# A hybrid decoder layer: input projection from a transposed copy of the input, with the norm factor applied to the projections

## The chip, the cores and the metric

The kernel runs on one core of a Trainium2 chip. A core has five engines with their own instruction queues: TensorE (PE; its weight loads are listed as PEld), VectorE (DVE), ScalarE (ACT), GpSimd (POOL), and SyncE (SP), which here issues most of the DMAs. They wait for each other through semaphores. The metric is the device time of one execution in microseconds (us), taken as the median of several runs.

## What is computed

One decoder layer on 1040 tokens (16 meta tokens ahead of 1024 inputs) of width 1024. The part that matters here is its beginning:

```python
def rmsnorm(x, g):
    y = x * lax.rsqrt(jnp.mean(x * x, axis=-1, keepdims=True) + EPS)
    return y * g

h = concatenate([meta, x], axis=1)
a = rmsnorm(h, ln_mix_pre)
proj = a @ w_in                         # 1024 x 3584
dq, dk, dv, hq, hf, hi, hg = split(proj)
y_diff = diff_attention(dq, dk, dv, ...)   # 4 heads, 128 columns of each kind a head
y_hgrn = hgrn2(hq, hf, hi, hg, ...)        # 4 heads, 128 columns of each kind a head
mix = concatenate([y_diff, y_hgrn]) @ w_out
h = h + rmsnorm(mix, ln_mix_post)
...                                     # convolutional FFN, then the output
```

The factor `rsqrt(mean(x*x) + EPS)` is one number for each token, and `g` one number for each of the 1024 input columns. So `(x * r * g) @ w` is the same as `((x * g) @ w) * r`, with `r` a factor for each token.

## The kernel before

**Precision.** Large products are made from numbers split in two: a high part (type fp32r) and the remainder. A product of two such numbers takes three matmuls: high by high, low by high, high by low. The normed, transposed input lies in SBUF as `ahi` and `alo`, 128 input columns on the partitions, eight such slices `k`, tokens along the row. A weight tile (128 columns of `w_in`) is loaded in two halves of 128x512 and split into `wh` and `wl`.

**Tokens.** They are divided into nine blocks (16 and eight times 128), and these into three groups of 272, 384 and 384 tokens (`GROUPS`). One projection of one kind for one group is 24 matmuls: eight slices by three products.

**Order.** TensorE executes its instructions strictly in the order in which the program writes them (`manual_schedule`). The other engines' instructions are placed by a scheduler ahead of time, which moves ready work forward; within the stretch in which `state["ordered"]` is true, each instruction of DVE, ACT and POOL is pinned behind the one written before it on its engine. `interleave` mixes a dense stream of projection matmuls with a side stream by estimated costs.

**The head** (lines 792 to 971). This is what happens before the loop over the heads:

- Token blocks are loaded as they are, tokens on the partitions. `pre_stat` (ACT) squares and sums each row and makes the factor by Ln and Exp; `pre_scale` (DVE) multiplies in the factor and the gain row `gb`, which two matmuls with a row of ones spread over the partitions (line 835). Blocks 4 and 5 are scaled on ACT and POOL (`far_block`).
- `pre_turn` transposes a block on TensorE, eight 128x128 pieces into two PSUM banks; `pre_hi` (ACT) copies them out as the high part, `pre_lo` (DVE) forms the remainder.
- `Kinds` does the projections of the first group of `dq`, `dk` and `dv` and the second group of `dq` in a hand-written order, among the transposes of blocks 3 to 5. `head0(1)` and `head0(2)` do the rest, with the transposes of blocks 6 to 8 and the four matmuls of the relative-position bias tables (`bias_tables`, line 353) as side streams.
- As a projection of a group ends, its `ev_...` function evacuates the PSUM bank. `ev_q` and `ev_k` split `q` and `k`: two ACT copies into the high parts of the halves, then two DVE remainders. `ev_v` (ACT) copies to `vt`, and `to_nat` later transposes `vt` back to tokens on the partitions.

**After the head** (lines 983 to 988) the loop over four head pairs mixes the projections of an HGRN head (`hf`, `hq`, `hi`, `hg`) with the attention of one head, then the projections of the next attention head with the work of the HGRN head. There `ev_f`, `ev_q`, `ev_i` and `ev_g` of `hgrn_in` evacuate; the transposes of `hi` and `dv` (`flush`) come 8 or 14 matmul steps after the group's end. In this loop two PSUM banks take the projections in turn. Output projection and FFN follow.

## Time and profile before

| | |
|---|---|
| median of 3 runs | 1275.59 us (1275.04 to 1276.89) |
| span of the profiled execution, first to last instruction | 1275.4 us |
| mean granted TensorE clock | 0.999 |
| weight load of the first `hf` matmul (the head is over) | 57.58 us |
| input and weights in flight by DMA | about 2 to 19.5 us |

The profiled execution's own time is known as its span; the median of the runs lies 0.2 us above it. In the profile a row in order of time gives start and duration in us, then engine, line, operation, written tile, read tiles, shapes and a count of merged instructions; in brackets stands the idle time of that engine before the row and what ended it. Most DVE, ACT and POOL instructions go through a helper at line 58 and are told apart by their tiles. Matmul durations include a pipeline tail that overlaps the next matmul, so their cost is read from start to start.

### The profile page before, as it was taken

To read this page: it belongs to the slowest core of one execution; us is meant where nothing else is said; L and a number is where in the kernel's file an instruction comes from. 1 tells how busy PE (TensorE), PEld (TensorE's weight loads), DVE (VectorE), ACT (ScalarE), POOL (GpSimd) and SP (SyncE) were. 2 spreads that over 40 slices of the span, in tenths; PEclk is the share of its full clock that TensorE was granted. 3 is DMA by queue.
4 is the path that set the end of the run, shared out by engine and by line. 5 is a ranking of instruction groups with operands and counts; after the bars stand their busy time and mean duration, and the time that the engine had idled before them with its cause. 6 is when DMAs were issued, how large, how long until landed. Compare 5 with 4: busy or idle time off the path is not lost.

```text
span 1275.4 us, 26064 instructions
## 1 busy us (share of the span) xinstructions
PE 1256.7 (99%) x10166; PEld 1172.8 (92%) x10166; DVE 913.9 (72%) x1492; ACT 687.3 (54%) x1638; POOL 507.2 (40%) x390
## 2 busy tenths in 40 slices
PE   8999999999999999999999999999999999999997
PEld 6999999999999998778899999999999998878886
DVE  7565646565656564457899888898898877797586
ACT  8475456546654754356764544445535445564554
POOL 5232423241323311353067676676776731020121
PEclk9999999999999999999999999999999999999999
DMA  7336555373734533787322221322222247955363
GB/s 260 96 60 131 89 139 94 83 146 92 132 94 79 125 82 113 232 279 253 131 67 67 92 88 63 100 76 75 92 75 83 75 116 258 351 184 173 91 215 124
DMA packets 116705, 165.04 MB, mean 129 GB/s; under 512 B 10131, under 2 KB 57811, under 8 KB 116582
## 3 DMA queue, kind: packets, MB, share of 16 engines
q1 hardware_dynamic: 93350, 151.84, 37.1%
q0 software_dynamic: 23232, 11.54, 7.7%
q8 instruction: 80, 1.31, 0.4%
q14 instruction: 43, 0.35, 0.1%
HBM read 134.24 MB, written 52.17 MB: 146 GB/s over the span
## 4 chain that ended last, share of the span: by engine, by line
PE 46%; DVE 4%; ACT 2%; issue 1%; POOL 1%; DMA 0%; SPq 0%; DVEq 0%; ACTq 0%; POOLq 0%
PE pd L1586 5%; PE pd L1587 5%; PE pd L1585 5%; PE pb L1412 4%; PE pb L1411 4%; PE pb L1413 4%; PE pc L1412 3%; PE pc L1411 3%; PE pc L1413 3%; PE pa L1412 3%; PE pa L1411 3%; PE pa L1413 3%; DVE xh L58 1%; DVE t L58 1%; DVE c L58 1%
## 5 line engine op out<-in xcount | busy, mean ns | idle before, releaser
L1412 PE MATMUL pb<-t,uh 128*128 128x258 f32 x504 | 141.0, 280 | 0.8 <-DVE t L58 0.8
L1411 PE MATMUL pb<-t,uh 128*128 128x258 f32 x504 | 140.5, 279 | 0.8 <-DVE u L58 0.8
L1413 PE MATMUL pb<-t,ul 128*128 128x258 f32 x504 | 140.2, 278 | 0.0
L1586 PE MATMUL pd<-wl,gh 128*128 128x512 f32 (+1 forms) x312 | 121.0, 388 | 1.1 <-DVE wl L58 1.1
L1585 PE MATMUL pd<-wh,gh 128*128 128x512 f32 (+1 forms) x312 | 120.8, 387 | 0.5 <-DVE x L58 0.5
L1587 PE MATMUL pd<-wh,gl 128*128 128x512 f32 (+1 forms) x312 | 120.7, 387 | 0.0
L58 DVE SCALAR_TENSOR_TENSOR c<-uu,cwt,c 128x514 f32<-128x514 f32 (+1 forms) x88 | 106.9, 1214 | 0.0
L58 DVE SCALAR_TENSOR_TENSOR c<-ug,cwt,c 128x514 f32<-128x514 f32 (+1 forms) x88 | 101.4, 1153 | 0.0
L1412 PEld LDWEIGHTS pb<-t,uh 128*128 128x128 f32 x504 | 94.8, 188 | 1.0 <-DVE t L58 1.0
L1411 PEld LDWEIGHTS pb<-t,uh 128*128 128x128 f32 x504 | 94.8, 188 | 1.0 <-DVE u L58 1.0
L58 ACT ACTIVATE c<-c 128x514 f32<-128x514 f32 (+1 forms) x44 | 27.9, 634 | 125.5 <-DVE c L58 125.5
L1413 PEld LDWEIGHTS pb<-t,ul 128*128 128x128 f32 x504 | 94.8, 188 | 0.0
L1412 PE MATMUL pc<-t,uh 128*128 128x258 f32 (+1 forms) x336 | 93.9, 279 | 0.0
L1412 PE MATMUL pa<-t,uh 128*128 128x258 f32 (+1 forms) x336 | 93.9, 279 | 0.0
L1411 PE MATMUL pa<-t,uh 128*128 128x258 f32 (+1 forms) x336 | 93.6, 278 | 0.0
L1411 PE MATMUL pc<-t,uh 128*128 128x258 f32 (+1 forms) x336 | 93.6, 278 | 0.0
L1413 PE MATMUL pc<-t,ul 128*128 128x258 f32 (+1 forms) x336 | 93.4, 278 | 0.0
L1413 PE MATMUL pa<-t,ul 128*128 128x258 f32 (+1 forms) x336 | 93.4, 278 | 0.0
L58 POOL TENSOR_TENSOR ul<-ws,uh 128x512 fp32r<-128x512 f32 x42 | 69.2, 1647 | 59.6 <-ACT uh L58 59.6
L58 POOL TENSOR_TENSOR ws<-ra,ra 128x512 f32<-128x512 f32 x42 | 67.9, 1617 | 60.9 <-DMA ra<-in_wup_dram 34.1
L58 POOL TENSOR_TENSOR c<-c,c 128x514 f32<-128x514 f32 (+1 forms) x44 | 68.8, 1564 | 53.9 <-ACT c L58 50.5
L58 DVE TENSOR_TENSOR ul<-ra,uh 128x512 fp32r<-128x512 f32 x43 | 41.5, 966 | 46.6 <-POOL ul L58 46.6
(389 smaller groups left out, 4183.1 us busy)
## 6 DMA issues: line engine op xcount, KB each, us to landing
ra<-in_wup_dram SPq DMA_DIRECT2D x88, 256.0 KB, 2.6
mp<-msc SPq DMA_DIRECT2D x23, 512.0 KB, 5.7
tsc<-in_wdown_dram SPq DMA_DIRECT2D x44, 256.0 KB, 5.2
wi<-tsc SPq DMA_DIRECT2D x44, 256.0 KB, 3.0
gi<-gsc SPq DMA_DIRECT2D x33, 256.0 KB, 4.2
wi<-in_wdown_dram SPq DMA_DIRECT2D x33, 256.0 KB, 5.2
gsc<-c SPq DMA_DIRECT2D x22, 257.0 KB, 2.1
tsc<-in_wdown_dram POOLq DMA_DIRECT2D x22, 256.0 KB, 7.2
```

The costliest lines, as they stand in the source:

```text
L58: ins = call(*args, **kw)
L1411: T.matmul(pt, hi[:, s], th[:, k], start=(first and k == 0), stop=False, skip_group_check=True)
L1412: T.matmul(pt, hi[:, s], tl[:, k], start=False, stop=False, skip_group_check=True)
L1413: T.matmul(pt, lo[:, s], th[:, k], start=False, stop=(k == 3), skip_group_check=True)
L1585: T.matmul(py, gh[:, s], wh, start=(k == 0 and pr not in (3, 7)), stop=False, skip_group_check=True)
L1586: T.matmul(py, gh[:, s], wl, start=False, stop=False, skip_group_check=True)
L1587: T.matmul(py, gl[:, s], wh, start=False, stop=(k == NH - 1), skip_group_check=True)
```

## The change

The host hands over a second copy of the input, `xt`: meta tokens and input together, transposed, 128 columns of the width on the partitions, one piece for each token group. The gain `gpre` comes laid out in columns. In the head:

- `load_xt` loads two halves of each group's piece (eight slices), the first group's ahead of and between the weights of `dq` and `dk`.
- `x_hi` (ACT) makes the high part directly from the raw input, times the gain of each input column (`gcol`, one number a partition), `x_lo` (DVE) the remainder. All block transposes, `pre_stat`, `pre_scale`, `far_block` and the broadcast of the gain row are gone.
- `x_squares` (ACT, in place, after both parts are made), `x_sum` (DVE, over the eight slices) and a matmul with a 128x128 tile of ones (`x_rstd`) put each token's sum of squares on all partitions; Ln and Exp make the factor `rs` for the group.
- Every evacuation, of all heads, multiplies by `rs`, on DVE. `ev_k`'s remainders and the gate product move to POOL; `ev_i` and `ev_v` move from ACT to DVE.
- The order by hand now covers more: all of the first two groups of the three kinds, 12 steps of the third, the evacuations of the first two groups, `smalls` and `lam_terms`.

The new parts of the diff, cut:

```diff
+    def x_hi(g, k):
+        return A.mul(ahi[:, k, xs_(g)], xr[g][:, k], gcol[:, k:k + 1])
+    def x_lo(g, k):
+        return V.scalar_tensor_tensor(alo[:, k, xs_(g)], xr[g][:, k], gcol[:, k:k + 1], ahi[:, k, xs_(g)].bitcast(F32), ALU.mult, ALU.subtract)
+    def x_squares(g, k0, k1):
+        A.activation(xr[g][:, k0:k1], xr[g][:, k0:k1], AF.Square)
+    def x_sum(g):
+        t0, t1 = span(g)
+        sq = zp.tile([P, 384], F32, tag="sq", name=f"sq{g}", bufs=2)[:, :t1 - t0]
+        V.tensor_reduce(sq, xr[g].rearrange("p k t -> p t k"), axis=AX.X, op=ALU.add)
+        return sq
+    def x_rstd(g, sq):
+        t0, t1 = span(g)
+        pt = ps_m(f"prs{g}")[:, :t1 - t0]
+        T.matmul(pt, ones, sq, start=True, stop=True)
+        return rstd_of(rs[:, t0:t1], pt, D)
...
         def ev_f(g, b0, b1, t0, t1, pt):
             fs = t["f"][:, t0:t1]
-            sigmoid(fs, t["kr"][:, t0:t1], pt)
+            V.tensor_tensor(fs, pt, rs[:, t0:t1], op=ALU.mult)
+            sigmoid(fs, t["kr"][:, t0:t1], fs)
...
-            A.mul(t["q"][:, t0:t1], pt, 128 ** -0.5)
+            V.scalar_tensor_tensor(t["q"][:, t0:t1], pt, 128 ** -0.5, rs[:, t0:t1], ALU.mult, ALU.mult)
...
-            A.copy(ht[:, : t1 - t0], pt)
+            V.tensor_tensor(ht[:, : t1 - t0], pt, rs[:, t0:t1], op=ALU.mult)
...
-            sigmoid(s, s, pt)
-            V.tensor_tensor(t["gate"][:, t0:t1], pt, s, op=ALU.mult)
+            gs = t["gate"][:, t0:t1]
+            V.tensor_tensor(gs, pt, rs[:, t0:t1], op=ALU.mult)
+            sigmoid(s, s, gs)
+            G.tensor_tensor(gs, gs, s, op=ALU.mult)
...
+        def scaled(nm, g, t0, t1, pt):
+            vt = ap_.tile([P, 384], F32, tag="vt", name=f"{nm}{h}_{g}", bufs=3)[:, : t1 - t0]
+            if nm == "qt":
+                V.scalar_tensor_tensor(vt, pt, 0.125, rs[:, t0:t1], ALU.mult, ALU.mult)
+            else:
+                V.tensor_tensor(vt, pt, rs[:, t0:t1], op=ALU.mult)
+            return vt
         def ev_q(g, b0, b1, t0, t1, pt):
+            qt = scaled("qt", g, t0, t1, pt)
             for m in range(2):
-                A.mul(qs[m][own[m], t0:t1], pt[own[m]], 0.125)
+                A.copy(qs[m][own[m], t0:t1], qt[own[m]])
...
+    state["ordered"] = True
+    for k in range(4):
+        x_hi(0, k)
+    w_hi(0, 0, G)
+    w_hi(1, 0, V)
+    for k in range(4):
+        x_lo(0, k)
+    w_lo(0, 0, G)
+    for k in range(4, KD):
+        x_hi(0, k)
+    w_hi(0, 1, G)
+    w_hi(1, 1, V)
+    for k in range(4, KD):
+        x_lo(0, k)
+    w_lo(0, 1, G)
+    w_lo(1, 0, G)
+    w_lo(1, 1, G)
+    w_hi(2, 0, A)
+    x_squares(0, 0, 4)
+    w_hi(2, 1, A)
+    x_squares(0, 4, KD)
+    w_lo(2, 0, V)
+    sq = x_sum(0)
+    w_lo(2, 1, G)
+    dq, dk, dv = first = [Kinds(j, 0, ps_in) for j in range(3)]
+    for half in range(2):
+        for a in (ahi, alo):
+            for kd in (dq, dk):
+                kd.part(half, 0, a)
+    for a in (ahi, alo):
+        for half in range(2):
+            dv.part(half, 0, a)
+    for kd in (dq, dk):
+        for half in range(2):
+            kd.part(half, 1, ahi)
+    for k in range(2):
+        x_hi(1, k)
+    x_rstd(0, sq)
+    for half in range(2):
+        dv.part(half, 1, ahi)
+    for k in range(KD):
+        if k > 1:
+            x_hi(1, k)
+        x_lo(1, k)
+    for k in range(KD):
+        x_hi(2, k)
+        x_lo(2, k)
+    second = [Kinds(j, 1, ps_m) for j in range(3)]
+    for k in range(KD):
+        for kd in second:
+            kd.mm(k, 0, ahi)
+            kd.mm(k, 1, ahi)
+    sums = {}
+    for g in (1, 2):
+        for c in range(2):
+            x_squares(g, 4 * c, 4 * c + 4)
+        if g == 1:
+            sums[1] = x_sum(1)
+            for kd in first:
+                kd.out()
+    for m in range(2):
+        G.memset(az[m], 0.0)
+    for kd in second:
+        for half in range(2):
+            kd.part(half, 0, alo)
+    third_group = head0()
+    for _ in range(12):
+        next(third_group)
+    x_rstd(1, sums[1])
+    for kd in second:
+        kd.out()
+    sums[2] = x_sum(2)
+    smalls()
+    lam_terms()
+    tables = bias_tables()
     state["ordered"] = False
...
+    interleave(third_group, [tables], 2600)
```

`kd.part(half, w, a)` is four matmuls of one kind with weight part `w` (0 high, 1 low) and input part `a`; `kd.out()` its evacuation. `head0()` runs the third group, 24 steps each of `dq`, `dk`, `dv`; it does a `to_nat` at step 20 of the first two, calls `x_rstd(2, sums[2])` at step 12 of `dk`, and from there on the third group's evacuations. `rs` takes the buffer X2, the raw first group X1, the raw weights of `dv` X0.

258 lines of the change are left out of this document (67 added, 191 removed).

## The prediction

> **What bounds the kernel now.** I read the page's totals first, then the stretches of the first 70 us, then the first 60 us row by row in time.
>
> ```profile
> span 1275.4 us, 26064 instructions
> PE 1256.7 (99%) x10166; PEld 1172.8 (92%) x10166; DVE 913.9 (72%) x1492; ACT 687.3 (54%) x1638; POOL 507.2 (40%) x390
> 0.00:10.00 10.00, 6.50 (x18) 3.80 (x19) 4.92 (x8) 7.23 (x16) 3.32 (x15) 1.00 0.71 247
> 10.00:20.00 10.00, 9.44 (x72) 8.72 (x70) 8.80 (x14) 9.12 (x21) 9.67 (x8) 1.00 0.98 364
> ...
> 30.00:40.00 10.00, 9.80 (x65) 8.85 (x64) 9.07 (x21) 7.58 (x22) 0.00 (x0) 1.00 0.01 2
> ...
> 60.00:70.00 10.00, 10.00 (x65) 9.70 (x66) 5.68 (x21) 6.93 (x25) 0.00 (x0) 1.00 0.14 44
> ```
>
> TensorE is busy 99% of the span at a granted clock of 1.00. In a row of stretches the columns are PE, PEld, DVE, ACT and POOL busy, clock, DMA share, GB/s. Only the first 40 us hold much idle TensorE time, and there DVE and ACT are nearly as full as TensorE. The rows of a fence are picked, not neighbours. From 40 to 500 us the stretches read like the last one. So the change can win only in the head, the projection of attention head 0, and can lose anywhere. TensorE executes in the written order, so the time is decided by when the head ends, the first weights of `hf`:
>
> ```profile
> 11.52 0.78 PE L901 MATMUL pi_dq<-ahi,wh_dq 128*128 128x272 f32 x4
> 57.58 0.19 PEld L248 LDWEIGHTS pi_hf<-ahi,wh_hf 128*128 128x128 f32 x1
> 14.03 0.66 PE L901 MATMUL pi_dk<-alo,wh_dk 128*128 128x272 f32 x4
> 14.52 0.66 PE L901 MATMUL pi_dk<-ahi,wl_dk 128*128 128x272 f32 x4
> 34.15 0.34 PE L250 MATMUL pi_dk<-alo,wh_dk 128*128 128x384 f32 x1
> 34.32 0.34 PE L252 MATMUL pi_dk<-ahi,wl_dk 128*128 128x384 f32 x1
> ...
> 16.69 1.03 PE L287 MATMUL px<-ident,xs 128*128 128x128 f32 x8
> L287 PE MATMUL px<-ident,xs 128*128 128x128 f32 x64 | 10.5, 309 | 2.0 <-DVE xs L58 1.4 <-POOL xs L58 0.6
> 53.31 0.34 PE L252 MATMUL pi_dv<-ahi,w 128*128 128x384 f32 x1
> 53.58 0.44 PE L353 MATMUL pb<-oh,tbb 64*128 64x384 f32 x1
> 53.95 0.44 PE L248 MATMUL pi_dv<-ahi,w 128*128 128x384 f32 x1
> 44.71 0.49 PE L369 MATMUL pn_va<-ident,vt 128*128 128x128 f32 x3
> 77.11 0.61 PE L746 MATMUL pa<-avn,at 128*128 128x128 f32 x4
> ```
>
> Projections run from 11.5 to 57.75 us. Start to start, a 272-column matmul takes 0.49 / 4 = 0.122 us and a 384-column one 0.17 (0.173 over longer runs); a block of eight transposes about 1.0; one bias-table matmul adds 0.64 - 0.17 = 0.47, one `to_nat` about 0.5.
>
> **What the change takes off TensorE.** All 64 transposes of full blocks (10.5 us in their row, about 8.3 start to start), the 8 small ones and the two broadcasts of `gpre` go. Three matmuls with `ones` come (f32; a plain 384-column matmul, 0.17, is the low end; two f32 ones of 128 columns took 0.61 in the L746 row, so at most 0.9 for 384; the pair of 512-column broadcasts below, at an idle TensorE, gives 1.4; I take 0.7, nearest to the L746 row, whose last matmul's tail is in the 0.61). The first projection can start when `x_hi(0, 0..3)` and the first weight half are there, near 6.4 us instead of 11.5. But the norm factor now needs a serial chain through ACT and DVE, priced next from these rows:
>
> ```profile
> 2.30 3.75 PE L835 MATMUL pg<-grow,ones 1*128 1x512 f32 x4 [2.30 <-DMA grow<-in_gpre_dram]
> 5.28 1.06 ACT L58 ACTIVATE xs<-xt 128x1024 f32<-128x1024 f32 x1 [0.37 <-DMA xt<-in_x_dram]
> 6.50:7.00 0.50, 0.14 (x2) 0.03 (x1) 0.28 (x1) 0.47 (x3) 0.00 (x0) 1.00 0.62 152
> 10.00:10.50 0.50, 0.50 (x5) 0.50 (x4) 0.50 (x2) 0.09 (x1) 0.33 (x1) 1.00 0.99 406
> 16.12 1.15 ACT L58 ACTIVATE xs<-X_in,ss 128x1024 f32<-128x1024 f32 x1
> 38.53 1.05 ACT L58 CAST k<-k 64x384 fp32r<-64x384 f32 x2
> 69.07 0.60 ACT L58 ACTIVATE kr<-kr,one 128x384 f32<-128x384 f32 x1
> 69.72 0.52 ACT L58 ACTIVATE f<-kr 128x384 f32<-128x384 f32 x1
> ...
> 69.65 0.50 DVE L58 SCALAR_TENSOR_TENSOR pb<-pb,ast 128x272 f32<-128x272 f32 x1
> 14.65 1.93 DVE L58 SCALAR_TENSOR_TENSOR xs<-X_in,ss,gb 128x512 f32<-128x512 f32 x2
> 16.50 1.50 DVE L58 CAST w<-X_in 128x512 fp32r<-128x512 f32 x1
> 16.11 1.60 POOL L58 TENSOR_TENSOR wl_dk<-X_in,wh_dk 128x512 fp32r<-128x512 f32 x1
> 38.66 1.12 DVE L58 TENSOR_TENSOR kl<-pi_dk,k 64x384 fp32r<-64x384 f32 x2
> 75.89 0.70 DVE L58 TENSOR_REDUCE ast<-S 128x1 f32<-128x528 f32 x1
> 97.57 1.11 DVE L58 TENSOR_REDUCE ast<-S 128x1 f32<-128x912 f32 x1
> ```
>
> **Start, up to the first sum (t0).** The bytes loaded are the same; their order is new. Before, 0.58 MB had landed at 5.28. The first half of group 0 is 0.56 MB and issued a little earlier: 5.0. At 406 GB/s, with the slow spell near 6.5 us kept, `dq`/`dk` half 0 come by 6.4, the second half of group 0 by 8.4, `dk` half 1 by 9.9. On DVE, `w_hi(1,1)` then runs beside a POOL subtraction, where such a copy took 1.50: 11.4. Four `x_lo` of 272 columns at 0.6 (0.50 alone, up to a third more beside POOL, as the 1.93 for two shows) end at 13.8. TensorE still has 37 matmuls (the last remainder, 4 + 16 + 16; 4.5 us) before the sum's own 0.5: **t0 = 18.8**, between 17.8 (no POOL beside DVE) and 19.6.
>
> The 1.93 row shows two-input DVE operations slowed by about a third beside POOL, and that is what I use. The Trainium skill ("SBUF — State Buffer", on the shared port pair) says more: such an operation and a GpSimd one shut each other out for the whole instruction. By it three POOL subtractions would stand between the four `x_lo`, and t0 would be 3.5 later; it is a rival below.
>
> **The chain behind t0.** ACT, DVE and POOL keep the written order here, so each term waits for the one before: Ln and Exp of group 0, 0.95 (0.60 and 0.52 at 384 columns, less for 272); 14 scaled copies `x_hi(1,2..7)`, `x_hi(2,0..7)` at 0.50 (the 1.15 row scaled to 384 columns, less 0.1 overlap), 7.0; `x_squares(1)`, twice 1536 columns, 2.9 (from 1.06 for 1024); `x_sum(1)`, 3072 elements, 3.4 (the two reduce rows give 1.05 ns an element); `qt` of group 0, 0.45; then ACT's two `q` copies, DVE's two remainders and `kt`, ACT's four `k` copies, 3.3 until ACT is free; `x_squares(2)`, 2.9; Ln and Exp of group 1, 1.1; group 1's evacuation on DVE, 3.25 (`qt`, wait for one copy, two remainders, `kt`, `vt`, by 1.12 for two); `x_sum(2)`, 3.4. Together about 28.7, with ten hand-overs at 0.05 **29.2: the third sum can start at 48.0**. TensorE gets through the rest of `dv` (8 x 0.122), group 1 (72 x 0.173) and, once `qt` has freed the first bank at 33.5, 37 steps of group 2 with a sum, two tables and one `to_nat` (8.5) by 42.0. There it waits 6.0, or waits part of it earlier for a PSUM bank. Behind it in its queue stand 35 projections (6.05), one `to_nat` (0.5), two bias tables (0.94), after the sum's 0.7: **head end 56.2**, against 57.75: 1.5 us won. TensorE's stream alone would end at 18.8 + 1.0 + 144 x 0.173 + 1.4 + 1.9 + 1.0 = 49.0 (sums, tables, two `to_nat`), 8.7 earlier than before; 7.2 of that go back to the chain.
>
> **After the head.** For every projection group one DVE multiplication (0.55 a 384-column op) takes over from ACT; `kl` and the gate product go to POOL. TensorE needs the result first in `to_nat`, 8 steps later:
>
> ```profile
> 180.20 0.47 ACT L58 COPY vt<-pi_dv 128x384 f32<-128x384 f32 x1
> 181.83 0.49 PE L369 MATMUL pn_va<-ident,vt 128*128 128x128 f32 x3
> PEld pi_dq L248 <- DVE gate L58: 0.9, 3, 0.3
> 26.78 0.15 DVE L58 TENSOR_SCALAR sub<-sub 128x1 f32<-128x1 f32 x1
> 27.46 0.41 DVE L58 CAST tbb<-tb 64x512 fp32r<-64x512 f32 x1
> ```
>
> In this group the copy ended 1.16 us before it was needed; one more DVE operation of 0.7 in front still fits. In exchange the 0.9 us of weight-load waits for the gate's slow evacuation should go. I take a net loss of 0.6, between a gain of 0.9 and a loss of 12 (third rival). Costing nothing: the later `az` fills (POOL is empty from 30 us already before), the small tensors' loads (queued on SP behind the big ones, used after 48 us), `rs` holding the X2 buffer until the last projection (its next user, a block load, needs head 3's output anyway); if that cover went, each would be a wait of a DMA's landing, about 2 to 5 us.
>
> Sum: 1275.4 - 1.5 + 0.6 = 1274.5; the median of the runs lies 0.2 above the span, so **1274.7**, within 0.2% (2.55 us, about what a measurement of this kernel can tell from no change).
>
> **Rivals.**
>
> *TensorE's stream binds, not the chain.* If the elementwise terms run 6 us shorter than priced, the sums arrive before TensorE asks, and the head ends between 49 and 54: 1267 to 1273, middle 1271. For it: the chain is some 35 instructions priced from neighbours. Against: DVE and ACT are 76 to 91% busy in the rows from 10 to 20 and 30 to 40 us already. Chance 0.26.
>
> *A bias table holds TensorE (slower).* `tables` stands in TensorE's queue at step 12 of `dq`, group 2, ahead of the third sum; its `tbb` copy (0.41, and 0.7 more) is not in the kept order. If it is placed behind `x_sum(2)` and the small vector work (some 16 operations like the 0.15 one, 2.6), the first table can start only at 51.7 and 60 projections, the other tables, `to_nat` and the sum (14) follow: 65.7, so 1283.5. It decides if `tbb` comes after 37 us. Against: before, `tbb` was put ahead at 27.46, among older work. Chance 0.08.
>
> *The evacuations wait in DVE's queue.* 21 groups feed a `to_nat`; where a DVE operation of over 0.7 us stands in front, TensorE waits, up to 0.6 each, 12 in all; at a third of that the time is 1278.5. For it: DVE is 72% busy over the span. Chance 0.09.
>
> *A slow restart.* After TensorE's idle first microseconds 20 transposes took 3.76 us (0.19 each); later eight took 1.03 (0.13).
>
> ```profile
> 7.83 3.76 PE L287 MATMUL px<-ident,xs 128*128 128x128 f32 x20 [1.19 <-DVE xs L58]
> ```
>
> If the 6 us wait brings that back for the 35 matmuls behind it, 0.46 x 6.05 = 2.8 is lost: 1277.5. The granted clock reads 1.00 in both stretches, so that row may as well have waited for data. Chance 0.08. The Trainium skill ("TensorE: Matmul & The Clock Gate", Part 1) has such a rule: an idle window of about 3.4 us halves the clock until a busy one has passed; the two rows agree in direction, not in the factor.
>
> *POOL shuts DVE out at the start.* DVE's four `x_lo` alternate with three subtractions of 1.3 us instead of losing 0.1 each: t0 is 3.5 later, and so is the whole chain: 1278.2. For it: the 1.50 copy, which ended with POOL's subtraction. Against: the 1.93 row. Chance 0.05. By the skill's rule on the port pair, named above, this is the case.
>
> **How the numbers follow.** Forecast 0.44, by its own errors (t0 by 1, the chain by 1.5) 1272 to 1277; of it 0.04 lies beyond the bound on the fast side and 0.01 on the slow one; of the slow restart and of the shut-out 0.02 each are slow. Faster 0.26 + 0.04 = 0.30; slower 0.08 + 0.09 + 0.01 + 0.02 + 0.02 = 0.22; same 0.48. The range, 1271.0 to 1279.5, leaves out half of the first rival and the bias-table case, about 0.2.
>
> **What would show it.** Right: first projection near 6.4 us; sums at about 18, 36 and 48 us; TensorE idle for some 6 us before the third; head end at 55 to 57; no TensorE waits beyond. Wrong: the third sum without a wait in front of it, a bias-table matmul after a long idle time, or idle TensorE time named after `vt` or `ht`.

## The result and the profile after

The changed kernel takes **1313.96 us** (median of 4 runs, 1310.53 to 1315.01); the kernel before took 1275.46 us beside it. The ratio is **1.029** (95% interval 1.028 to 1.031): 38 us slower, where 1274.7 was predicted, with a range up to 1279.5. The span of the profiled execution went from 1275.4 to 1312.5 us, 37.1 more.

The totals of the changed kernel's page:

```profile
span 1312.5 us, 25924 instructions
PE 1262.2 (96%) x10096; PEld 1177.4 (90%) x10096; DVE 951.8 (73%) x1534; ACT 672.3 (51%) x1582; POOL 534.9 (41%) x421
```

TensorE has 70 matmuls fewer and is busy 5.5 us longer; 31.6 us are new idle time. Where they arose is read from the view of one tile, which gives for each group of instructions the shortest, median and longest duration in ns, and the first and the last start. Here are the groups of the changed kernel that begin a stage: `hf` (the head is over), `py` (output projection), `pc` and `pd` (the two halves of the FFN).

```profile
L248 PE MATMUL pi_hf<-ahi,wh_hf x96: 283/335/445, 72.6 to 464.6; 128*128 128x384 f32 x64, 128*128 128x272 f32 x32
L996 PE MATMUL py<-woh,mp x119: 387/394/796, 523.8 to 649.0; 128*128 128x512 f32 x119
L1376 PE MATMUL pc<-t,uh x336: 275/280/290, 681.9 to 1091.1; 128*128 128x258 f32 x84, 128*128 128x256 f32 x84
L1550 PE MATMUL pd<-wh,gh x312: 278/389/501, 1091.5 to 1305.4; 128*128 128x512 f32 x152, 128*128 128x256 f32 x4
```

The same groups of the kernel before:

```profile
L248 PE MATMUL pi_hf<-ahi,wh_hf x96: 282/336/445, 57.8 to 438.2; 128*128 128x384 f32 x64, 128*128 128x272 f32 x32
L1031 PE MATMUL py<-woh,mp x119: 387/389/500, 496.6 to 616.5; 128*128 128x512 f32 x119
L1411 PE MATMUL pc<-t,uh x336: 275/278/283, 649.4 to 1055.2; 128*128 128x258 f32 x84, 128*128 128x256 f32 x84
L1585 PE MATMUL pd<-wh,gh x312: 277/389/504, 1055.5 to 1268.3; 128*128 128x512 f32 x152, 128*128 128x256 f32 x4
```

| stage | rows used | before | after | more |
|---|---|---|---|---|
| head | start to first `hf` | 57.8 | 72.6 | 14.8 |
| loop over the heads | first `hf` to first `py` | 438.8 | 451.2 | 12.4 |
| output projection | first to last `py` | 119.9 | 125.2 | 5.3 |
| between | last `py` to first `pc` | 32.9 | 32.9 | 0 |
| first half of the FFN | first `pc` to first `pd` | 406.1 | 409.6 | 3.5 |
| rest | first `pd` to the end | 219.9 | 221.0 | 1.1 |

So there is not one loss but four: the head, the loop, the output projection and the FFN. (The last row's 1.1 is within what this stage varies by itself: 218.7 to 221.3 us over all the kernels below.)

**The head.** The changed kernel's waits of TensorE up to 72.6 us (us in total, times, longest):

```profile
PE prs L298 <- DVE lmx L58: 10.3, 1, 10.3
PE pi_dq L834 <- POOL wh_dq L58: 6.5, 1, 6.5
PE pi_dq L248 <- DVE qt L58: 3.3, 1, 3.3
PE pi_dq L834 <- DVE alo L58: 2.9, 3, 1.0
```

And some of its stretches, with the columns that the prediction names:

```profile
16.00:18.00 2.00, 1.44 (x6) 1.45 (x7) 1.43 (x3) 1.46 (x2) 0.21 (x1) 0.50 1.01 377
44.00:46.00 2.00, 2.00 (x5) 0.77 (x3) 0.00 (x0) 1.95 (x4) 1.54 (x4) 0.50 0.00 0
50.00:60.00 10.00, 1.73 (x9) 1.34 (x8) 9.71 (x8) 4.12 (x8) 6.28 (x6) 0.83 0.38 113
62.00:64.00 2.00, 1.93 (x4) 1.35 (x5) 1.52 (x12) 0.49 (x2) 0.00 (x0) 0.50 0.00 0
```

From 50 to 60 us TensorE did 1.7 us of work while DVE was busy for 9.7. And after each of the waits for `alo`, `qt` and the third sum there are stretches with a granted clock of 0.50. The rows of DVE, POOL, ACT and TensorE behind this, from the view in order of time:

```profile
10.70 5.80 DVE L58 SCALAR_TENSOR_TENSOR alo<-xr,gcol,ahi 128x272 fp32r<-128x272 f32 x4
11.89 2.90 POOL L58 TENSOR_TENSOR wl_dk<-wr_dk,wh_dk 128x512 fp32r<-128x512 f32 x2
23.90 0.62 PE L298 MATMUL prs<-sq,ones 128*128 128x272 f32 x2
25.47 7.19 ACT L58 ACTIVATE ahi<-xr,gcol 128x384 fp32r<-128x384 f32 x14
32.57 2.85 ACT L58 ACTIVATE xr<-xr 128x1536 f32<-128x1536 f32 x2
35.46 5.47 DVE L58 TENSOR_REDUCE sq<-xr 128x384 f32<-128x3072 f32 x1 [0.81 <-ACT xr L58]
48.64 0.52 ACT L58 ACTIVATE rs<-rs 128x384 f32<-128x384 f32 x1
50.23 0.56 DVE L58 COPY rb<-pb 128x384 f32<-128x384 f32 x1 [2.98 <-PE pb L345]
52.58 3.04 DVE L58 TENSOR_TENSOR q<-qt,q 64x384 fp32r<-64x384 f32 x2
56.58 5.34 DVE L58 TENSOR_REDUCE sq<-xr 128x384 f32<-128x3072 f32 x1
62.07 1.62 PE L298 MATMUL prs<-sq,ones 128*128 128x384 f32 x2 [10.34 <-DVE lmx L58]
```

A `x_lo` beside POOL's subtractions took 1.45 us (5.80 / 4). The third sum stands behind `x_sum(2)`; it waited 10.3 us for it (the bracket names `lmx`, the small instruction that follows the reduction on DVE; the releaser is inferred).

**The loop.** The changed kernel's waits of TensorE between 80 and 525 us:

```profile
PE pl L469 <- DVE hq L58: 3.5, 3, 1.4
PE pu L526 <- ACT kn L58: 2.3, 3, 0.9
PE pa L747 <- DVE at L58: 1.4, 4, 0.6
PE pl L469 <- DVE am L58: 1.4, 1, 1.4
PE E L666 <- ACT pb L58: 1.4, 3, 0.5
```

Together 10.0 of the 12.4 us; in the kernel before, the same view from 60 to 497 us has no row at all. None is named after `vt` or `ht`, where the prediction looked. They stand in the side streams: the HGRN's and attention's own products wait for DVE and ACT steps that now come later.

**The output projection and the FFN.** The changed kernel as `py` begins, in order of time, on DVE, SyncE and TensorE:

```profile
523.97 0.56 DVE L58 TENSOR_TENSOR gate<-pi_hg,rs 128x384 f32<-128x384 f32 x1 [2.27 <-PE pi_hg L252]
524.56 1.19 SPq L1024 DMA_DIRECT2D mp<-msc  x2
528.96 0.80 PE L996 MATMUL py<-woh,mp 128*128 128x512 f32 x1 [3.63 <-DMA mp<-msc]
529.98 0.63 PE L1000 MATMUL py<-woh,mp 128*128 128x512 f32 x1
530.41 0.63 PE L996 MATMUL py<-woh,mp 128*128 128x512 f32 x1
```

And a pair of loads with this name of the kernel before:

```profile
453.84 1.19 SPq L1059 DMA_DIRECT2D mp<-msc  x2
```

A block tile is loaded in two parts, the first two of them into X1 and X2. Before, the first part of X2's block went out at 422.6 and its second part in the pair at 453.84, with the second of X1's: all of it 43 us ahead of the first `py` (496.6). Now both parts of X2's block go out as the last reader of `rs` ends, at 524.5. TensorE stands 3.6 us for it and then runs at 0.43 a matmul instead of 0.23, for 5 us. In the FFN TensorE waits for nothing new, but its `pc` matmuls have a median of 280 ns instead of 278: the loss is in the pace.

### The profile page after: what moved, and what is told of

Its sections match the earlier page's. It is cut to its first block, busy times and chain, and to the rows that moved or that the text cites. A ratio compares the mean times of both kernels' runs of the same rounds, so it can differ in the third digit from the quotient of the medians.

```text
span 1312.5 us, 25924 instructions
## 1 busy us (share of the span) xinstructions
PE 1262.2 (96%) x10096; PEld 1177.4 (90%) x10096; DVE 951.8 (73%) x1534; ACT 672.3 (51%) x1582; POOL 534.9 (41%) x421
## 4 chain that ended last, share of the span: by engine, by line
PE 42%; DVE 4%; DMA 3%; ACT 2%; issue 1%; POOL 1%; SPq 1%; DVEq 0%; POOLq 0%
PE pb L1377 4%; PE pb L1376 4%; PE pb L1378 4%; PE pd L1551 4%; PE pd L1552 3%; PE pd L1550 3%; PE pc L1377 3%; PE pc L1378 3%; PE pc L1376 3%; PE pa L1377 3%; PE pa L1376 3%; PE pa L1378 3%; DMA gi<-gsc 2%; DMA gc<-gsc 1%; DVE xh L58 1%
## 5 line engine op out<-in xcount | busy, mean ns | idle before, releaser
L58 POOL TENSOR_TENSOR ws<-ra,ra 128x512 f32<-128x512 f32 x42 | 64.4, 1533 | 62.0 <-DMA ra<-in_wup_dram 50.7
```

Source lines behind the costliest of these rows:

```text
L58: ins = call(*args, **kw)
```

## The experiments

The experiments are single runs but for n2, n4 and n5, each beside the kernel before on the same chip (1275.15 to 1277.88); stages are read from the tile view as above. How far a stage varies by itself can be read from kernels in which it is the same: the loop of the changed kernel took 451.2 to 452.9 us (after, e3, e4, e5, e8, e9), its output projection 123.7 to 125.5, the old loop 438.7 to 438.9 (before, e1, e2, n1, n2, n5; e2 has one added evacuation). "e" starts from the changed kernel, "n" takes its transposed input but norms it before it is split.

| kernel | time | head end | loop | `py` stage | `pc` to `pd` |
|---|---|---|---|---|---|
| before | 1275.5 | 57.8 | 438.8 | 119.9 | 406.1 |
| after | 1314.0 | 72.6 | 451.2 | 125.2 | 409.6 |
| e1_loop_plain | 1293.4 | 71.9 | 438.8 | 117.8 | 409.7 |
| e2_last_scaled | 1300.5 | 72.2 | 438.9 | 125.2 | 409.6 |
| e3_sums_te | 1296.0 | 56.7 | 451.8 | 124.1 | 409.6 |
| e4_fillers | 1310.0 | 68.3 | 452.2 | 125.5 | 409.7 |
| e5_swap | 1311.7 | 71.5 | 452.4 | 123.7 | 409.6 |
| e6_columns | 1302.5 | 57.0 | 456.2 | 118.1 | 417.8 |
| e7_pool_to_dve | 1303.8 | 61.2 | 450.3 | 126.7 | 409.7 |
| e8_start | 1292.7 | 51.0 | 452.1 | 124.9 | 409.6 |
| e9_places | 1310.9 | 72.3 | 452.9 | 124.7 | 406.0 |
| e10_q_plain | 1292.7 | 56.4 | 448.3 | 124.9 | 409.6 |
| e11_q_in_psum | 1301.3 | 56.0 | 455.2 | 126.1 | 409.6 |
| n1_normed_first | 1287.1 | 67.5 | 438.7 | 119.2 | 406.2 |
| n2_normed_early | 1281.3 | 63.4 | 438.9 | 117.7 | 406.2 |
| n4_sums_ahead | 1278.2 | 54.5 | 444.3 | 118.9 | 406.1 |
| n5_tables_apart | 1276.8 | 55.3 | 438.9 | 121.8 | 406.2 |

### The evacuations, and the last of them

`e1_loop_plain` gives every evacuation after the head its old form, without the factor:

```diff
-            V.tensor_tensor(ht[:, : t1 - t0], pt, rs[:, t0:t1], op=ALU.mult)
+            A.copy(ht[:, : t1 - t0], pt)
...
-            V.tensor_tensor(gs, pt, rs[:, t0:t1], op=ALU.mult)
-            sigmoid(s, s, gs)
-            G.tensor_tensor(gs, gs, s, op=ALU.mult)
+            sigmoid(s, s, pt)
+            V.tensor_tensor(gs, pt, s, op=ALU.mult)
```

> The head is as in the changed kernel; every evacuation after it (HGRN heads, attention heads 1 to 3) is as it was before the change, so the norm factor is left out there and the factor's buffer is free from the end of the head. Theory (the evacuations on DVE and POOL cost the loop over the heads 12.3 us, and the late release of the factor's buffer costs the output projection 5.3): the stretch from the first hf matmul to the first output projection, 451.2 us in the changed kernel and 438.8 before, comes back to 439; the 3.6 us wait of the output projection for a block of the mixed output goes; head end unchanged at 72.6; total about 1314.0 - 12.3 - 5.3 = 1296. Rival (the later stages lose because everything is shifted against the weight loads, not because of the evacuations): the stretch stays at 451 and the total at 1314.

`e2_last_scaled` is e1 with the factor left in one evacuation only, that of the last gate group of the last head:

```diff
+            if (h, g) == (HEADS - 1, 2):
+                V.tensor_tensor(gs, pt, rs[:, t0:t1], op=ALU.mult)
+                sigmoid(s, s, gs)
+                G.tensor_tensor(gs, gs, s, op=ALU.mult)
+                return
```

> As the run with plain evacuations after the head, but the last gate evacuation of all (head 3, third token group) keeps its multiplication by the factor on DVE and its gate product on POOL; the factor is left out elsewhere after the head. This is one more reader of the factor's buffer, about 500 us later. Theory (the wait in the output projection is the buffer's release, followed by a block load of 4.4 us): the output projection loses its 5.3 us again, 3.6 as a wait and the rest at half clock behind it, total about 1301.7. Rival (that load is late because of other traffic or of the whole loop): no wait, total as in the other run.

With e1 the loop is back at 438.8, and the wait for `mp` is gone: the loop's loss is the evacuations', all of it. One single late reader of `rs` brings that wait back and makes e2 7.1 us slower than e1. The view of waits of e2, from 72 to 640 us, has it as its first row:

```profile
PE py L1021 <- DMA mp<-msc: 3.6, 1, 3.6
```

So "`rs` holding X2 costs nothing" was wrong: 3.6 us of waiting, and about as much again at the low clock behind it and in what was put off.

### The sums

`e3_sums_te` leaves the sums over the eight slices of groups 1 and 2 to TensorE: eight fp32r matmuls with `ones` accumulate the squares in PSUM, in place of the DVE reduction.

```diff
-        T.matmul(pt, ones, sq, start=True, stop=True)
+        if sq is not None:
+            T.matmul(pt, ones.bitcast(F32), sq, start=True, stop=True)
+        else:
+            for k in range(KD):
+                T.matmul(pt, ones, sqs[g][k // 5][:, k % 5], start=(k == 0), stop=(k == KD - 1))
...
-            sums[1] = x_sum(1)
-    sums[2] = x_sum(2)
```

> The sums of squares of token groups 1 and 2 are made on TensorE: eight fp32r matmuls with the ones take the squares of the eight slices, and DVE's two reductions of 5.4 us are gone; all else as in the changed kernel. Theory (the two reductions stand in the chain that ends in the third sum, and the waits drag the clock down): the waits of 3.3 and 10.3 us go, and with them some 4 us of half-clock matmuls; 16 matmuls of 0.173 come for two f32 ones of 0.7. Head end 72.6 - 13.6 - 4 + 1.4 = 56.4, total about 1298. Rival (evacuations and their hand-overs between ACT and DVE bind as much as the reductions): a wait of 3 us or more is left before a matmul of the third group, head end 60 or later.

The head ends at 56.7, 15.9 earlier, and in the view of waits of e3 up to 57 us neither the wait for `qt` nor that before the third sum is left. There remain the one before the first projection, 0.4 us for `wh_dk`, and these:

```profile
PE pi_dq L847 <- DVE alo L58: 2.8, 3, 1.0
PE pn_va L374 <- DVE vt L58: 0.5, 1, 0.5
```

Taking 10.8 us of reductions off DVE saved 15.9: they carried the 3.3 and the 10.3 us waits, and with the waits went the slow matmuls behind them.

### The clock

`e4_fillers` keeps every wait's cause and fills the waiting time with matmuls whose result nobody reads: ahead of the first projection, between the four `dq` matmuls that wait for remainders, ahead of the third group and ahead of the third sum. Cut:

```diff
+    filler(p1, 17, parts[0][0][0][:, :P], ahi[:, 0, xs_(1)])
     third_group = head0()
...
-                    x_rstd(2, sums[2])
+                    x_rstd(2, sums[2], None, 54)
```

> Extra matmuls whose result is overwritten stand in TensorE's queue in the places where it was idle in the head: 14 before the first projection, 6 between each two of the four dq matmuls that wait for DVE's remainders, 17 before the third group, 54 before the third sum. Nothing else changes. Theory (after idle stretches TensorE ran at half clock, 0.32 us a 384-column matmul for 0.173): those stretches run at full pace, the first sum comes at 21.6 for 23.9, the third some 2 us earlier, and the head ends 4 to 5 us earlier, at 68; total 1309. Rival (the slow matmuls wait for operands that come late, and the clock has no part in it): pace as before, head end 72.6 or later.

The stretch from 10 to 70 us of e4:

```profile
10.00:70.00 60.00, 55.82 (x324) 51.37 (x325) 46.48 (x65) 33.13 (x60) 19.23 (x23) 1.00 0.38 132
```

The clock of this stretch of e4 reads 1.00 where the changed kernel's falls to 0.50, and the head ends 4.3 us earlier though TensorE has more to do. This is the price of the low clock in the head, or its least value: in e4 a new wait of 1.8 us, for `vt`, stands before the first `hf`. The Trainium skill ("TensorE: Matmul & The Clock Gate", Part 1) has it that an idle window of some 3.4 us halves the clock; the trace agrees, down to the factor of two that the prediction doubted: 0.50 granted, 0.43 a `py` matmul instead of 0.23. In the changed kernel three waits of about 1 us in a row, with little work between, were enough.

The clock column does not show everything. In the changed kernel these four matmuls followed on others without a wait, and the next began at 11.10:

```profile
10.19 1.11 PE L834 MATMUL pi_dk<-alo,wh_dk 128*128 128x272 f32 x4
```

That is 0.23 us each, about half pace, while the column reads 1.00 from 10 to 11 us. In e4, behind the matmuls put ahead of the first projection, the same four took 0.125 each. So the opening runs slow too after TensorE's first idle microseconds, and a column of 1.00 there does not speak against it. In the changed kernel this cost nothing by itself, as TensorE then waited for `x_lo` anyway.

### The start

`e8_start` is e3 with the weight remainders of `dq` and `dk` on DVE, behind the four `x_lo`, so that POOL subtracts nothing beside them, and with the first sum on TensorE as well:

```diff
-    w_lo(0, 0, G)
     for k in range(4, KD):
         x_hi(0, k)
...
-    w_lo(0, 1, G)
-    w_lo(1, 0, G)
-    w_lo(1, 1, G)
...
+    for c in range(2):
+        for j in range(2):
+            w_lo(j, c, V)
```

> On top of the run with the sums on TensorE: the four weight remainders of dq and dk go from POOL to DVE, behind DVE's input remainders, and the first group's sum of squares too is made by TensorE. Theory (POOL's subtractions shut out DVE's four input remainders, 1.45 us each for 0.55, and the waits halve the clock): these four take 2.2 us in all, no wait of 1 us between the dq matmuls, first sum at 18.5 (23.7 there), head end 51.5 (56.7 there). The FFN's weight remainders lie as before the change, so 3.5 us less there if that is their cause; total 1287.5, else 1291. Rival (the elementwise chain behind the first sum binds, not TensorE): head end 54 or later with waits named after alo or vt.

The head ends at 51.0, 5.7 before e3, and TensorE's waits for `alo` are gone (only its first, 6.3 us, and 0.5 for a `vt` are left). This is 6.8 us less than the head before. So the transposed input does free the head, by 6.8 of the 8.7 us that TensorE's stream alone promised; the changed kernel lost it in how the norm's chain was laid.

### What of the evacuations costs the loop

`e10_q_plain` is e3 with the old `q` evacuation in heads 1 to 3 (the factor is left out there); `e7_pool_to_dve` is e3 with the two products that the change gave to POOL back on DVE; `e11_q_in_psum` is e3 with `q`'s factor written back into PSUM, so that the remainders read one operand from PSUM.

```diff
+            if h:
+                for m in range(2):
+                    A.mul(qs[m][own[m], t0:t1], pt[own[m]], 0.125)
...
-            G.tensor_tensor(gs, gs, s, op=ALU.mult)
+            V.tensor_tensor(gs, gs, s, op=ALU.mult)
...
-            qt = scaled("qt", g, t0, t1, pt)
+            qt = pt
+            V.scalar_tensor_tensor(pt, pt, 0.125, rs[:, t0:t1], ALU.mult, ALU.mult)
```

> On top of the run with the sums on TensorE: in attention heads 1 to 3 the q projection is evacuated as before, without the factor, which is left out of q there: two ACT copies from PSUM, two DVE remainders from PSUM. Theory (the dq stretches of heads 1 and 2 lose 3.3 and 1.2 us because the remainders now wait in DVE's queue for DVE's own multiplication and then ACT, with the HGRN level behind them, and read two SBUF operands beside POOL): the dq stretches go from 18.8 and 16.7 to 15.5 each, first hf to first output projection from 451.8 to 447; total 1291. Rival (the HGRN levels are late because of the multiplications of the kinds ahead of dq): 451 and 1296.

> On top of the run with the sums on TensorE: the remainders of k and the gate products go back from POOL to DVE, everywhere; the multiplications by the factor stay. Theory of the loop's loss (DVE's queue is too long): DVE has about 20 operations of 0.5 to 0.6 more a head, first hf to first output projection goes from 451.8 to 455 or more; total 1299 or more. Rival (POOL's new work shuts DVE out): the stretch shrinks to 446 or less, total 1290.

> On top of the run with the sums on TensorE: DVE's multiplication of q by the factor writes back into the PSUM bank instead of an SBUF tile, so that ACT's copies and DVE's remainders read PSUM, as before the change; the number of DVE instructions and their order are the same. Theory A (the remainders lose because both their inputs are in SBUF, so that POOL's instructions shut them out; a DVE instruction with one SBUF input is not held): no remainder of q takes over 0.6, the dq stretches of heads 1 and 2 go from 18.8 and 16.7 to 16 or less. Theory B (the loss is the place in DVE's queue, behind DVE's own multiplication and ACT's copy): they stay within 0.5 of 18.8 and 16.7. The dq stretches before the change took 15.5.

e10: the loop goes from 451.8 to 448.3, near the expected 447; `q` alone costs 3.5 us in three heads. The `dq` stretches of heads 1 and 2 went from 18.8 and 16.7 to 16.6 and 15.1. In its view of waits the time that TensorE stands for `hq` has gone from 3.5 to this:

```profile
PE pl L476 <- DVE hq L58: 1.3, 2, 0.8
```

e7 missed on both sides: 1.5 us better in the loop, hardly more than a loop varies by itself, and neither the 3 worse of a fuller DVE queue nor the 6 better of a freed POOL. On balance it hardly matters where these two products stand; as both went back together, a gain of one and a loss of the other may hide in it. (Its head came out at 61.2; `kl` went back to DVE there too.)

e11 was to separate two ways in which the `q` factor may hurt. Its remainders, read from PSUM, never took more than 0.56 us; in e3, with both operands in SBUF, the longest took 1.55 (in the head; 1.39 in the loop). The tile view of `q` in e3:

```profile
L58 DVE TENSOR_TENSOR q<-qt,q x24: 434/552/1552, 35.6 to 402.4; 64x384 fp32r<-64x384 f32 x16, 64x272 fp32r<-64x272 f32 x8
```

The same in e11:

```profile
L58 DVE TENSOR_TENSOR q<-pi_dq,q x24: 433/551/560, 34.9 to 405.3; 64x384 fp32r<-64x384 f32 x16, 64x272 fp32r<-64x272 f32 x8
```

And TensorE's longest wait in the loop of e11:

```profile
PE pl L482 <- DVE hq L58: 6.2, 4, 2.0
```

So DVE and POOL do shut each other out where DVE reads two operands from SBUF, as the Trainium skill says ("SBUF — State Buffer", Who interferes with whom); both traces agree with it. Yet the loop of e11 is 3.4 us longer, not shorter, and TensorE waits 6.2 us for `hq` instead of 3.5. The `dq` stretches of heads 1 and 2 came to 20.1 and 17.2, where theory A had 16 or less for both and theory B 18.8 and 16.7 within 0.5. The reason is that the edit also changed the hand-over from ACT. The same group's remainders in e3 and in e11:

```profile
268.31 1.14 DVE L58 TENSOR_TENSOR q<-qt,q 64x384 fp32r<-64x384 f32 x2 [0.58 <-ACT q L58]
268.59 1.12 DVE L58 TENSOR_TENSOR q<-pi_dq,q 64x384 fp32r<-64x384 f32 x2 [1.03 <-ACT q L58]
```

In e3 the first remainder begins when ACT's first copy is done, in e11 only after both: DVE idles 9.8 us for these copies instead of 5.7. So the longer loop is of e11's own making, and its time does not decide between the theories. What the shut-out of these remainders takes in the loop is read from their sum: the 18 of the loop take 10.7 us in e3 and 9.4 in e11, so it is 1.3 us of DVE's time in three heads. The rest of the 3.5 us that e10 won fits the longer chain DVE, ACT, DVE that stands in front of the HGRN's `hq`; no run isolates it.

`e6_columns`, also on e3, moved the factor of `hi` and `dv` (heads 1 to 3) behind the turn, where a token is a partition and the ACT copy can take it for nothing, and that of `hq` into the later norm:

```diff
-            V.tensor_tensor(ht[:, : t1 - t0], pt, rs[:, t0:t1], op=ALU.mult)
+            A.copy(ht[:, : t1 - t0], pt)
...
+            for j in range(n):
+                A.mul(dst[:, j0 + j], pt[:, P * j: P * (j + 1)], rc[:, j0 + j:j0 + j + 1])
```

> On top of the run with the sums on TensorE: after the head, hi and dv leave PSUM by an ACT copy as before, and the factor is applied when to_nat copies their transposes out (ACT, one factor a partition); hq leaves PSUM on ACT without the factor, which goes into the eps of the norm behind it; in head 3 hi is projected last, so that the factor's buffer is free one kind earlier. That is 27 DVE operations of 0.55 less in the loop over the heads, for nine tiny matmuls. Theory (DVE's queue causes the loop's waits, and the release of the buffer those of the output projection): first hf to first output projection matmul 451.8 goes to about 444 (438.8 before the change), and the wait of 3.6 for a block of the mixed output and its half-clock matmuls go; total 1296 - 7 - 5.5 = 1283. Rival (POOL's new work, kl and the gate products, holds DVE up through the shared port): the stretch stays at 450 or more.

It missed by 19 us, in two places; only the output projection came out as expected, at 118.1 without the wait for `mp`. The factor as a column is made by small matmuls in the first `hf` group. They took 1.9 us, the wait for `vt` ahead of them 2.2 instead of e3's 1.2, and behind them the clock reads 0.64 from 66 to 69 us, so that this stretch of `hf` took 21.1 us instead of 16.4. The loop is 4.4 longer than in e3, though the excess of `hi` and `hg` went; `q` was left as it was, and TensorE still waits 3.5 us for `hq`. And the FFN took 8 us more, which led to the next pair.

### The FFN's pace

Nothing of the FFN is touched by the change. `e5_swap` exchanged two POOL remainders so that the low weight halves lie in the buffers that they had before; `e9_places` only takes the buffers X0, X1 and X2 in the order in which the kernel before takes them first, and with this gives them their old places in SBUF.

```diff
-    rs = mix_tile("X2", F32, "rs")[:, :L]
+    raw2 = mix_tile("X0", F32, "raw2")
...
+    rs = mix_tile("X2", F32, "rs")[:, :L]
     def span(g):
```

> The changed kernel with two POOL instructions of the head in the other order: the remainder of dk's first weight half ahead of that of dq's second half, as before the change. The buffers for weight remainders then rotate as before, and the FFN's remainders of w_up lie where they lay before; 38 of 147 of them lie one buffer off in the changed kernel. Theory (the FFN's 3.5 us have nothing to do with the factor or with waits, but with where these tiles lie in SBUF): from the first pc to the first pd matmul 405.8 us as before, not the 409.2 of the changed kernel; all else as there; total about 1310.5. Rival (the FFN is slower for another reason, such as the raw sums' buffers or DMA): 409 again, total 1314.

> The changed kernel with one thing different: the three shared buffers X0, X1 and X2 are first taken in the order of before the change, so that they lie at their old addresses in SBUF (in the changed kernel X2, with the factor, comes first and the transformed input that the FFN's matmuls read lies elsewhere). Theory (the FFN's 3.5 us are the place of the operands that its matmuls stream): first pc to first pd 405.8 us as before the change, for 409.2 in the changed kernel; all else as there, total 1310.5. Rival (the place of these buffers has no part in it): 409 and 1314.

The first row of `pc` of e5:

```profile
L1376 PE MATMUL pc<-t,uh x336: 275/280/289, 680.5 to 1089.7; 128*128 128x258 f32 x84, 128*128 128x256 f32 x84
```

Of e9:

```profile
L1377 PE MATMUL pc<-t,uh x336: 275/278/283, 682.8 to 1088.5; 128*128 128x258 f32 x84, 128*128 128x256 f32 x84
```

And of e6, whose added constants and smaller `vt` pool move other tiles of SBUF too:

```profile
L1417 PE MATMUL pc<-t,uh x336: 277/282/298, 664.2 to 1081.6; 128*128 128x258 f32 x84, 128*128 128x256 f32 x84
```

409.2, 405.7 and 417.4 us from first to last, for the same matmuls. The weight buffers' theory fell with e5. The places of X0 to X2 account for the whole 3.5 us, and the four n kernels, which have the old places, take 406.1 or 406.2 from `pc` to `pd`. Which property of a place it is was not settled. That e6's 8 us are of the same kind is likely, but was not tried alone.

### Norm first: what the transposed input is worth

If the factor is the whole of the loop's loss, it should be multiplied in once, at the input, ahead of the split. `n1_normed_first` does this: group by group it squares, sums on TensorE, norms on DVE, splits, and projects; all evacuations are those of the kernel before, and X0 to X2 have their old places.

```diff
+    def x_norm(g, k):
+        t0, t1 = span(g)
+        V.scalar_tensor_tensor(xr[g][:, k], xr[g][:, k], gcol[:, k:k + 1], rs[:, t0:t1], ALU.mult, ALU.mult)
...
     def x_hi(g, k):
-        return A.mul(ahi[:, k, xs_(g)], xr[g][:, k], gcol[:, k:k + 1])
+        A.copy(ahi[:, k, xs_(g)], xr[g][:, k])
```

> Another kernel on the transposed input: squares of a group (ACT), their sum over the slices and partitions by eight matmuls with ones, the factor, and then DVE multiplies gain and factor into the input slice before it is split; all evacuations as before the change. No transposes of blocks, no factor behind the projections, X0 to X2 in their old places. By the theories so far the loop over the heads (438.8), output projection, FFN and end are as before; the head is DVE's two operations a slice (48 at 0.45 to 0.55) beside TensorE's 216 projections, 24 sum matmuls and tables: first projection at 10.5 to 11, head end 50.5 if TensorE binds, 55 if DVE does; total 1268 to 1273. Rival (the elementwise chain binds as in the changed kernel): head end above 58, total above 1276.

1287.1: the loop (438.7) and the FFN (406.2) are those of before, and the loss is in the head alone (67.5), with 6.2 us of waiting for the squares of a group, and a clock of 0.57 from 46 to 58 us. `n2_normed_early` squares each group while the one before is projected, advances `dq` and `dk` of the third group together, ahead of `dv`, moves weight remainders from POOL to DVE and puts matmuls whose result nobody reads ahead of the first projection. The part on the squares and sums of group 1:

```diff
+        if k < 4:
+            x_squares(1, 2 * k, 2 * k + 2)
...
+        if k == 5:
+            x_total(1)
+        if k == 6:
+            x_rstd(1)
```

> The kernel that norms the transposed input before it splits it, with three things mended that its first trace showed: the sums of groups 1 and 2 stand earlier in TensorE's queue (TensorE waited 2.7 and 1.7 us for the factors and then ran at half clock), the weight remainders of the head are all on DVE but one (POOL held DVE's two-operand instructions to 0.96 and 1.53 us for 0.50), dq and dk of the third group advance slice by slice together, and matmuls whose result is overwritten keep TensorE busy before the first projection. Evacuations and everything after the head as before the change. If TensorE binds: first projection at 11 to 12, 216 projections 34, sums, tables and transposes 7, head end 51 to 53 (57.8 before the change, 67.5 in the first trial), total 1269 to 1271. Rival (DVE's 48 operations and evacuations bind): head end 55 to 57, total 1273 to 1275.

It took 1281.34 us (1280.95 to 1284.23, 5 runs; ratio 1.004, 1.003 to 1.005): the head end of 63.4 missed both theories. Two rows of its ACT, whose instructions are pinned in the written order here, show why:

```profile
38.03 0.58 ACT L58 ACTIVATE raw<-prs,eps 128x384 f32<-128x384 f32 x1 [3.70 <-PE prs L307]
43.45 0.52 ACT L58 COPY avn<-pn_va 16x128 f32<-16x128 f32 x2 [3.48 <-PE pn_va L373]
```

It stood 3.7 us before a root whose sum TensorE came to late, and 3.5 before a turn, while slices of group 2 that TensorE wanted were queued behind. `n4_sums_ahead` changes only these places:

```diff
-        if k == 5:
+        if k == 3:
             x_total(1)
...
-    to_nat(*late.pop(0))
     x_norm(2, 0)
...
-        if k in (1, 3, 5):
-            second[k // 2].out()
+        if k >= 5:
+            second[k - 5].out()
```

> Built on n2_normed_early (input normed before the split, evacuations as before): the sums of groups 1 and 2 stand after the fourth instead of the sixth column in TensorE's order, the root of group 2 stands after the seventh column of group 1, group 2's columns stand ahead of group 1's evacuations and of the first turn of v on ACT and DVE. Theory (in n2 the order of the chain, and not its length, holds the head at 63.4): ACT no longer stands 3.7 us before the root of group 2, nor 3.5 us before the turn, TensorE is fed from 24 us on without a wait over 0.5 us, group 2 starts near 37 to 39 and the head ends at 52 to 55, the loop stays 438.9, the time is 1268 to 1272, below the kernel before. Rival (the chain's length holds it: two more DVE passes over every column, 1.17 us a column): DVE is still late for each column of group 2, the head ends at 58 or later and the time is 1274 or more.

The head ends at 54.5, 3.3 before the kernel before; the order, not the length of the chain, had held it. But the loop gave 5.5 back (1278.23 us, 1275.32 to 1281.99, 12 runs; ratio 1.001, 0.9998 to 1.0023). In its view in order of time, the fourth bias table on DVE and the scores on TensorE:

```profile
61.48 0.56 DVE L58 COPY rb<-pb 128x384 f32<-128x384 f32 x1 [5.20 <-DMA rsc<-rb]
62.09 0.34 PE L668 MATMUL S<-k,q 128*128 128x144 f32 x1 [3.60 <-DVE rb L58]
```

The tables shared one buffer, each waiting until the one before was written out; with the head shorter the scores now came first. `n5_tables_apart` gives them a place each in X2:

```diff
+        rbs = mix_tile("X2", F32, "rb4")
...
-            rb = zp.tile([P, 384], F32, tag="rb", name=f"rb{h}", bufs=1)
+            rb = rbs[:, 384 * h:384 * h + 384]
```

> Built on n4_sums_ahead: the four bias tables get a place each instead of one that each takes over from the one before. In n4 the head ends at 54.5, 3.3 before that of the kernel before, but the first scores wait 3.6 us for the fourth table, whose place comes free only when the one before it has been written out, and the projections behind that wait run at half pace. Theory (that wait is the whole loss of the loop in n4): no wait over 1 us is left between 50 and 120 us, the loop takes 439 to 440, the time is 1270 to 1272, below the kernel before by 0.3 to 0.4%. Rival (the tables' copies stand behind the columns of group 2 on DVE anyway, and the scores only wait for something else next): the loop stays above 442 and the time above 1273.5.

The wait for the table is gone (one of 1.6 us, for `vt`, is left ahead of the first `hf`) and the loop is at 438.9, as expected. The time is not the 1270 to 1272 expected: 1276.83 us (1273.59 to 1278.49, 12 runs) against 1277.62 of the kernel before on that chip, a ratio of 0.9986 (0.9976 to 0.9997). By the medians that is 0.8 us faster, below the 0.2% that the prediction set as the limit of what can be told. Of the 2.5 us won in the head the profiled execution loses 1.9 in the output projection, where its view of waits has two that are smaller in n4 (1.4 and 0.4):

```profile
PE ss L594 <- DVE on L58: 1.8, 1, 1.8
PE pl L480 <- issue: 1.4, 1, 1.4
```

These were not pursued.

## Why the prediction was wrong, step by step

**The head: 56.2 predicted, 72.6 measured.** The plan of the chain was right, its sizes were not.

- *First projection 6.4:* measured 6.50.
- *t0, 18.8:* the first sum ended at 24.5. Two terms, about half each. The four `x_lo` "at 0.6" took 1.45 each and ended at 16.5 instead of 13.8: the rival "POOL shuts DVE out at the start", given 0.05, was the case. And the 37 matmuls behind them with the sum took 8.0 us instead of 5.0, at a clock of 0.50 up to 22 us: the rival of the slow restart, given 0.08, in a place where it was not looked for. What was held against it, that the granted clock read 1.00 in both of its rows, was no evidence, as the opening of the changed kernel and e4 show.
- *The chain, 29.2:* measured 62.07 - 24.5 = 37.6. The copies (7.19 for 7.0) and squares (2.85 for 2.9) were priced well. Mis-sized was `x_sum`: 5.4 instead of 3.4, twice. The rate of 1.05 ns an element came from the difference of two reductions over consecutive elements, each to one sum; this one makes 384 sums over eight slices, with a stride. By the same reckoning, from 3.94 us for 2176 elements and 5.47 for 3072, it costs 1.71. Then 1.9 for the `q` remainders of group 1, in 3.04 instead of 1.12 beside POOL's weight remainders (51.13 to 55.21), and 1.5 for `qt`, whose factor was ready at 49.16 and which stood behind a table's copy on DVE. That is 7.4 of the 8.4; the rest is in smaller terms.
- *TensorE waits 6.0 before the third sum:* it waited 10.3 there and 3.3 earlier. The place was right.
- *Third sum to head end, 8.2:* it took 10.6, at a clock of 0.50 up to 66 us.

The trace shows where these terms stand; that the reductions bind was shown by e3, the clock by e4, the start by e8.

**After the head: a net loss of 0.6 predicted, 22.3 measured.** This is the step that failed in its reasoning.

- The check "does the copy to `vt` still arrive before its turn" was right: no wait is named after `vt` or `ht`. But it was the wrong question. TensorE's strict order also holds the products of the HGRN and of the attention, and these wait for DVE and ACT steps (`hq`, `am`, `kn`, `at`) that were pushed back. The rival "the evacuations wait in DVE's queue" had DVE's queue right, but its 12 us were counted for waits before `to_nat`, of which there were none; that the loop lost 12.4 is chance. How they divide among the kinds was found for `q` alone (3.5, e10). DVE's busy share of 72% over the span said nothing on this; the side streams' slack at each product would have.
- "`rs` holding the X2 buffer costs nothing" failed. The argument was that X2's next user needs the output of head 3 anyway. The 453.84 row refutes it: even the last part of that load had been going out 43 us before the last projection ended, and the whole was now held to the end of the last gate evacuation. The stage lost 5.3, by e2 up to 7; the "2 to 5 us" given for the case that the cover went was nearer.
- The 3.5 us of the FFN were in no step: a change of the order in which buffers are first taken was not seen as a change of their places.

**The rivals that did not come:** the bias table was placed early (its `tbb` ended before `x_sum(1)`), and TensorE's stream did not bind in the changed kernel. It came nearest in e8, whose head end of 51.0 lies in that rival's 49 to 54.

**The idea.** That a factor that commutes with a product may be moved behind it is right, but the price differs: ahead of the split it is one pass over 8 slices of three groups, in the head; behind, it is 84 evacuations, each on a path that others wait for. Moved back (n5), with the transposes still gone, the kernel is level with the one before or a hair faster.

## What to carry to other kernels

Where TensorE executes a fixed order of interleaved streams, price an added step on another engine by what stands behind it in that engine's queue for every stream, not only for its own; a queue at 72% can still be late at each product. Before reusing a dead buffer for something that lives long, find out when its next user's load is issued now, not when its result is needed. And when a wait is removed, expect the next one to come with little room: in n4 and n5 the win of one stage was handed to the next until it was looked for.

## What the runs showed of the hardware

- A DVE reduction to 384 sums over eight strided slices took 5.47 us for 3072 elements, one to 272 sums 3.94 for 2176: 1.71 ns for each further element, against 1.07 in the kernel before for reductions of consecutive elements to one sum (1.11 us for 912, 0.70 for 528). Whether the stride or the number of short sums makes the difference was not tried.
- Low clock after short waits: three waits of 0.85 to 1.03 us for `alo` (2.9 together, the last before 16.56) were enough for a granted clock of 0.50 from 16 to 22 us.
- The clock column read 1.00 at the changed kernel's first matmuls, though they ran at half pace (0.23 us each for 272 columns; 0.125 in e4).
- DVE operations with two operands in SBUF took up to three times as long beside POOL subtractions (1.45 us for an `x_lo`, 0.43 without; 1.55 for a `q` remainder in e3, at most 0.56 in e11 with one operand in PSUM).
- The pace of matmuls depended on where their operands lie in SBUF: `pc` took 405.7 or 409.2 us for the same work, with only the places of X0 to X2 changed (e9, after).
